# A decoder step on one core: raw weight halves loaded two weights ahead, in a ring of four

## The chip, the core and the metric

The kernel runs on one core of a Trainium2 chip. The metric is the device time of one execution in microseconds; the verdict on a change goes by the median of several. Engines are named as in the profile: PE is TensorE, DVE is VectorE, ACT is ScalarE, POOL is GpSimd, and SP is SyncE, which here issues every DMA.

## What is computed

One inference step of a decoder with two layers, for a prompt of 1024 tokens and 8 sample sequences of 4 tokens each, 1056 columns in all, with a model width of 1024. Layer 0 is a gated linear recurrence, layer 1 an attention over keys and values that three groups of heads share; each is followed by the same MLP. Everything is in float32.

```python
for layer in range(DEPTH):                      # DEPTH = 2
    if layer < N_A_LAYERS:
        h, s_fin = _hgrn2(_rmsnorm(x, a_norm[layer]), a_w_in[layer], ...)
    else:
        kv = _rmsnorm(x, kv_norm) @ w_kv        # keys, values of 3 groups
        q = _rmsnorm(x, b_norm[j]) @ b_w_q[j]   # 3 groups x 8 heads x 128
        ...
        h = o @ b_w_o[j]
    x = x + h
    x = x + jnp.square(jax.nn.relu(_rmsnorm(x, mlp_norm[layer]) @ mlp_w_up[layer])) @ mlp_w_down[layer]
```

The MLP's inner width is 4096.

## The kernel before, in words

**Weights.** A weight here is a tile of 1024 x 128 numbers, in SBUF 128 partitions x 8 x 128. `weight_order` lists all 212 of them in the order of their use. A product is made three times over (`mm3`, lines 185 to 187, and `mmx`, lines 805 to 807): each operand is split into a high part that TensorE takes as it is and a low part that holds the rest, and high x high, high x low and low x high are summed in PSUM. So each weight has to be prepared before use. `_prep` (line 125) allocates its pair `whi` and `wlo` from the pool `wp`, which has two buffers of each, loads the raw weight in two halves of 256 KB (line 146, tiles `wraw`, a ring of two), multiplies them by a norm gain for the projections of the attention (line 148, on POOL), copies each half into `whi` (line 131, on ACT) and subtracts on POOL to get `wlo` (line 132).

**When a weight is made.** `wnext` hands out the weight that is due and sees to it that this one and the next have been prepared (`wahead`). So weight i+1 is prepared when weight i begins to be used. The tracing order isn't the order on the chip: at the end a list scheduler puts every engine's instructions in an order, by priorities and by its own estimate of when operands will be there. `_prep` runs with a priority 400 instructions ahead of its place. On the chip each engine takes its queue strictly in that order and waits where an operand is late.

**The MLP.** `mlp` (line 700) goes in eight groups of 512 inner columns. For each it makes four weights `up` (`proj`, three chunks of 384, 384 and 288 columns: chunks 0, 1 and 2 below) and evacuates each chunk by a chain in `ev_up`: ReLU from PSUM on ACT (line 720), square on DVE (line 721), for some chunks differences of such results (lines 726 and 743, DVE), and the split into high and low part (line 709 on ACT, line 710 on DVE or POOL). Each group's four weights `down` come after the first `up` of the next group. For seven of the eight groups of a layer these products are made for two column chunks at a time with seven half products in place of eight (`down`, line 809), which needs sums and differences of quarters of the weight and of the hidden values. Such weights are marked `two`. Their `_prep` adds lines 152 to 165, with a priority 20 ahead: three sums on DVE (lines 159 to 161), one on POOL (line 162) into two tiles `wsum` (two buffers in all), and their split into `whix` and `wlox` (two buffers of each, in the pool `wx`), again by lines 131 and 132. Line 159 reads the second raw half.

**Inside `down`.** TensorE makes a product into the PSUM tile A, then into C and B, then comes back to A. Before it may write A again, DVE must have added A into the residual `xr` (line 819, `add(0, 0, A)`); the same holds later for the other tiles. The last group of a layer uses plain products (lines 788 to 797).

**Other users of weights.** `phase_a` (line 288) begins with the loads of the input in three chunks and prepares weights 0, 1 and 2 between them (line 293); it computes the norm, the projections and, in lanes that are stepped by `tick`, the recurrence. `phase_c` (line 860) projects keys, values and queries, attends, merges and projects back.

Of the kernel before, what the change touches and what calls it, by code (L numbers as in the profile page):

```python
# [10 lines left out]
F32 = mybir.dt.float32  # L11
# [7 lines left out]
P = 128  # L19
# [27 lines left out]
class Kern:  # L47
    def __init__(self, nc, tc, aps, ctx):
        self.nc, self.tc, self.a, self.ctx = nc, tc, aps, ctx
        self.const = ctx.enter_context(tc.tile_pool(name="const", bufs=1))  # L50
        self.rs = ctx.enter_context(tc.tile_pool(name="rs", bufs=2))
        self.op = [self.const.tile([P, KD, NT], F32R, name=n) for n in ("opH", "opL")]
        self.chunks = CHUNKS
        self.wp = ctx.enter_context(tc.tile_pool(name="wp", bufs=2))
        self.pp = ctx.enter_context(tc.tile_pool(name="pp", bufs=4, space=PSUM))
        self.pg = ctx.enter_context(tc.tile_pool(name="pg", bufs=4, space=PSUM))
        self.wx = None
        self.wt = {}
        self.wi = 0
        self.wq = self.weight_order()  # L60
        self.queue, self.lanes = deque(), []
        self.merged = 0
        self.every, self.ticks = 0, 0
        self.rawx = False
        self.fine = False
# [30 lines left out]
    def weight_order(self):  # L96
# [25 lines left out]
        mlp(1)  # L122
        return q

    def _prep(self, i):
        nc = self.nc
        src, gi, x, *two = self.wq[i]
        pool, s = (self.wx, "x") if x in (True, "p") else (self.wp, "")

        def pair(hi, lo, j, raw):  # L130
            nc.scalar.activation(hi[:, j:j + 4, :], raw, AF.Copy)  # L131
            nc.gpsimd.tensor_tensor(lo[:, j:j + 4, :], raw, hi[:, j:j + 4, :].bitcast(F32), op=ALU.subtract)  # L132

        with self.tc.high_priority(offset=400 if i > 1 else 0):
            if x == "q":

                hi, lo = (self.cp.tile([P, NP_], F32, name="q", bufs=6).bitcast(F32R).rearrange("p (k m) -> p k m", m=P)
                          for _ in range(2))
            else:
                hi = pool.tile([P, 8, P], F32R, name="whi" + s)  # L140
                lo = pool.tile([P, 8, P], F32R, name="wlo" + s)
            raws = []
            for j in (0, 4):
                raw = (self.wx if x is True and self.rawx else self.wp).tile([P, 4, P], F32, name="wraw")
                raws.append(raw)
                nc.sync.dma_start(raw, src[:, j:j + 4, :])
                if gi is not None:
                    nc.gpsimd.tensor_tensor(raw, raw, self.gains[:, gi, j:j + 4][:, :, None].to_broadcast([P, 4, P]), op=ALU.mult)  # L148
                pair(hi, lo, j, raw)
            self.wt[i] = (hi, lo)  # L150
        if two:
            with self.tc.high_priority(offset=20):

                sh = self.wx.tile([P, 8, P], F32R, name="whix")
                sl = self.wx.tile([P, 8, P], F32R, name="wlox")
                (a11, a12), (a21, a22) = ((r[:, :2], r[:, 2:]) for r in raws)
                t, u = (self.wx.tile([P, 4, P], F32, name="wsum") for _ in range(2))
                tt = nc.vector.tensor_tensor
                tt(t[:, :2], a21, a22, op=ALU.add)  # L159
                tt(t[:, 2:], t[:, :2], a11, op=ALU.subtract)  # L160
                tt(u[:, :2], a11, a21, op=ALU.subtract)
                nc.gpsimd.tensor_tensor(u[:, 2:], a12, t[:, 2:], op=ALU.subtract)  # L162
                pair(sh, sl, 0, t)
                pair(sh, sl, 4, u)
                self.wt[i] = (hi, lo), (sh, sl)
# [6 lines left out]
    def wnext(self):  # L172
        i = self.wi
        self.wi += 1
        self.wahead(i)
        self.wahead(i + 1)
        return self.wt.pop(i)


# [1290 lines left out]
```

## Time and profile before

| | us |
|---|---|
| median of 3 runs | 3045.53 |
| lowest and highest run | 3034.98, 3046.78 |
| the profiled execution | 3045.13 |
| its span, first to last instruction | 3043.4 |
| TensorE busy in the span | 2875.0 (94%) |
| VectorE, ScalarE, GpSimd busy | 1796.0, 1282.9, 1338.3 |
| mean granted TensorE clock | 0.989 of full speed |

The rows come from the profiled execution, so sums over its rows are made against its own 3045.13 us; the median lies 0.40 above. Times in timelines count from the start of the span. Busy time of an engine says how much work lies on it, and not what another engine waits for; that is read from the waits and the timelines. TensorE's matmuls overlap each other, so a matmul's row lasts longer than the distance to the next one.

### The profile page before, as it was taken

What the parts mean: (1) busy time and instruction counts of PE and PEld (TensorE: products, weight loads), DVE (VectorE), ACT (ScalarE), POOL (GpSimd) and SP (SyncE); (2) the same over time, 40 slices, a digit from 0 to 9 for tenths busy, and PEclk for the clock granted to TensorE, in tenths of its full rate; (3) what the DMA queues carried; (4) which work ended last, traced back from release to release, by engine and by line L of the source; (5) the groups of instructions that cost most, each with busy time, mean ns of one, the idle gap of its engine ahead of it and who ended that gap; (6) DMA issues with size and microseconds to landing.
All of it is one profiled execution on the core that took longest, in us unless ns stands there. A gap on an engine that the chain in (4) does not pass through costs nothing.

```text
span 3043.4 us, 47407 instructions
## 1 busy us (share of the span) xinstructions
PE 2875.0 (94%) x18144; PEld 2757.8 (91%) x18144; DVE 1796.0 (59%) x3467; ACT 1282.9 (42%) x2972; POOL 1338.3 (44%) x1149
## 2 busy tenths in 40 slices
PE   6998999889999999999899999999999999999999
PEld 5888888889999999999899889889888999999999
DVE  8777777876544455543654565665676455544442
ACT  6555656643332222332445544555544223332221
POOL 5444444453544444544463553333225445444442
PEclk9999999999999999999999999999999999999999
DMA  3100211230111111112212233332641111111112
GB/s 113 36 30 30 71 40 29 69 123 18 46 49 43 49 46 46 49 43 63 84 62 68 84 99 108 124 117 71 195 150 42 44 48 49 42 46 46 49 49 86
DMA packets 131956, 201.92 MB, mean 66 GB/s; under 512 B 26320, under 2 KB 65872, under 8 KB 129680
## 3 DMA queue, kind: packets, MB, share of 16 engines
q1 hardware_dynamic: 131728, 198.88, 20.9%
q8 instruction: 143, 2.34, 0.3%
q14 instruction: 85, 0.70, 0.1%
HBM read 164.04 MB, written 34.80 MB: 65 GB/s over the span
## 4 chain that ended last, share of the span: by engine, by line
PE 56%; DVE 10%; POOL 8%; issue 7%; DMA 5%; ACT 3%; POOLq 0%; SPq 0%; DVEq 0%; ACTq 0%
PE pj L185 10%; PE pj L186 10%; PE pj L187 10%; POOL wlo L132 4%; PE pj L805 4%; PE pj L806 4%; PE pj L807 4%; DMA wraw<-w_dn 3%; PE g L806 2%; PE g L805 2%; PE g L807 2%; POOL wlox L132 2%; PE g L1143 2%; PE g L1115 1%; PE g L1130 1%
## 5 line engine op out<-in xcount | busy, mean ns | idle before, releaser
L185 PE MATMUL pj<-opH,whi 128*128 128x352 f32 (+2 forms) x3408 | 1136.7, 334 | 9.9 <-DVE xr L211 3.5
L186 PE MATMUL pj<-opL,whi 128*128 128x352 f32 (+2 forms) x3408 | 1110.1, 326 | 5.0 <-POOL opL L233 3.2
L187 PE MATMUL pj<-opH,wlo 128*128 128x352 f32 (+2 forms) x3408 | 1107.0, 325 | 2.9 <-POOL wlo L132 2.7
L132 POOL TENSOR_TENSOR wlo<-wraw,whi 128x512 fp32r<-128x512 f32 x404 | 546.5, 1371 | 913.1 <-ACT whi L131 882.1
L185 PEld LDWEIGHTS pj<-opH,whi 128*128 128x128 f32 x3408 | 645.8, 190 | 30.6 <-issue 16.9
L186 PEld LDWEIGHTS pj<-opL,whi 128*128 128x128 f32 x3408 | 646.7, 190 | 17.9 <-POOL opL L233 6.6
L187 PEld LDWEIGHTS pj<-opH,wlo 128*128 128x128 f32 x3408 | 645.6, 189 | 6.9 <-POOL wlo L132 4.1
L131 ACT ACTIVATE whi<-wraw 128x512 fp32r<-128x512 f32 x404 | 232.6, 621 | 546.6 <-PE g L806 439.9
L721 DVE TENSOR_TENSOR tmp<-tmp 128x384 f32<-128x384 f32 (+1 forms) x192 | 169.5, 883 | 311.2 <-ACT tmp L720 311.2
L819 DVE TENSOR_TENSOR xr<-xr,pj 128x384 f32<-128x384 f32 x336 | 183.7, 553 | 138.5 <-PE pj L807 138.3
L496 POOL TENSOR_TENSOR lv<-b 128x512 f32<-128x512 f32 x112 | 125.0, 1127 | 102.7 <-PE g L593 58.4
L720 ACT ACTIVATE tmp<-pj 128x384 f32<-128x384 f32 (+1 forms) x192 | 86.9, 453 | 189.3 <-PE pj L187 188.5
L132 POOL TENSOR_TENSOR wlox<-wsum,whix 128x512 fp32r<-128x512 f32 x112 | 151.0, 1368 | 0.6 <-ACT whix L131 0.6
L162 POOL TENSOR_TENSOR wsum<-wraw,wsum 128x256 f32<-128x256 f32 x56 | 43.7, 781 | 168.0 <-DVE wsum L160 153.8
L1117 DVE CUSTOM_DVE_ANT_0 pr<-g,band,rq 128x128 f32<-128x128 f32 (+1 forms) x192 | 67.9, 405 | 79.9 <-PE g L1115 76.3
L1120 ACT ACTIVATE pr<-pr,nm 128x128 f32<-128x128 f32 (+1 forms) x192 | 84.1, 440 | 68.0 <-DVE nm L1118 67.8
L148 POOL TENSOR_TENSOR wraw<-wraw,gains 128x512 f32<-128x512 f32 x72 | 91.4, 1275 | 40.0 <-DMA wraw<-w_q 33.3
L211 DVE TENSOR_TENSOR xr<-xr,pj 128x384 f32<-128x384 f32 (+1 forms) x132 | 67.2, 516 | 69.7 <-PE pj L187 37.5
L709 ACT ACTIVATE hbH<-tmp 128x384 fp32r<-128x384 f32 x106 | 54.9, 526 | 121.2 <-DVE tmp L721 72.8
L967 POOL TENSOR_TENSOR q<-q,cos 32x512 f32<-32x512 f32 x48 | 89.8, 1877 | 30.2 <-DVE rsw L966 28.9
L159 DVE TENSOR_TENSOR wsum<-wraw 128x256 f32<-128x256 f32 x56 | 23.8, 425 | 131.5 <-DMA wraw<-w_dn 131.3
L806 PE MATMUL g<-hL,whi 128*128 128x288 f32 x336 | 100.5, 299 | 0.0
(399 smaller groups left out, 5917.8 us busy)
## 6 DMA issues: line engine op xcount, KB each, us to landing
wraw<-w_up SPq DMA_DIRECT2D x128, 256.0 KB, 2.8
wraw<-w_dn SPq DMA_DIRECT2D x128, 256.0 KB, 2.8
wraw<-w_in SPq DMA_DIRECT2D x64, 256.0 KB, 2.8
wraw<-w_q SPq DMA_DIRECT2D x48, 256.0 KB, 2.9
ub<-us SPq DMA_DIRECT2D x32, 256.0 KB, 2.2
cc<-ck SPq DMA_DIRECT2D x8, 1024.0 KB, 5.1
cc<-cv SPq DMA_DIRECT2D x8, 1024.0 KB, 5.4
wraw<-w_kv SPq DMA_DIRECT2D x24, 256.0 KB, 2.9
```

The costliest lines, as they stand in the source:

```text
L131: nc.scalar.activation(hi[:, j:j + 4, :], raw, AF.Copy)
L132: nc.gpsimd.tensor_tensor(lo[:, j:j + 4, :], raw, hi[:, j:j + 4, :].bitcast(F32), op=ALU.subtract)
L148: nc.gpsimd.tensor_tensor(raw, raw, self.gains[:, gi, j:j + 4][:, :, None].to_broadcast([P, 4, P]), op=ALU.mult)
L185: nc.tensor.matmul(ps, wh[:, kw, :], xh[:, kx, :], start=(i == 0), stop=False)
L186: nc.tensor.matmul(ps, wh[:, kw, :], xl[:, kx, :], start=False, stop=False)
L187: nc.tensor.matmul(ps, wl[:, kw, :], xh[:, kx, :], start=False, stop=(i == len(ks) - 1))
L496: nc.gpsimd.tensor_tensor(r(lv), r(b), r(b)[:, :, h - 1:h].to_broadcast([P, 256 // h, 2 * h]), op=ALU.subtract)
L721: nc.vector.tensor_tensor(r, r, r, op=ALU.mult)
L805: nc.tensor.matmul(ps, wh[:, kw, :], xh, start=start and i == 0, stop=False, skip_group_check=True)
L806: nc.tensor.matmul(ps, wh[:, kw, :], xl, start=False, stop=False, skip_group_check=True)
L807: nc.tensor.matmul(ps, wl[:, kw, :], xh, start=False, stop=stop and i == len(items) - 1, skip_group_check=True)
L819: self.nc.vector.tensor_tensor(x(i, c), x(i, c), ps, op=ALU.add)
```

## The change

The ring of raw halves has four buffers instead of two, in whichever pool it is taken from. The loading of a raw weight moves out of `_prep` into `_load`, which is called from two places: from `_prep`, where it hands out halves that were loaded before or loads them, and from `wnext`, which now loads the raw halves of weight i+2, with a priority 400 ahead, when it hands out weight i. Weights that carry a mark for another pool (the third field of their entry: `True`, `"p"` or `"q"`) are not loaded ahead. Nothing else in the preparation of a weight changes: the copies, subtractions, sums and their priorities stay where they are.

```diff
@@ -55,7 +55,7 @@
         self.wx = None
-        self.wt = {}
+        self.wt, self.raw = {}, {}
         self.wi = 0
@@ -122,6 +122,17 @@
+    def _load(self, i):
+
+        if i in self.raw:
+            return self.raw.pop(i)
+        src, _, x = self.wq[i][:3]
+        raws = []
+        for j in (0, 4):
+            raws.append((self.wx if x is True and self.rawx else self.wp).tile([P, 4, P], F32, name="wraw", bufs=4))
+            self.nc.sync.dma_start(raws[-1], src[:, j:j + 4, :])
+        return raws
+
     def _prep(self, i):
@@ -139,11 +150,8 @@
-            raws = []
-            for j in (0, 4):
-                raw = (self.wx if x is True and self.rawx else self.wp).tile([P, 4, P], F32, name="wraw")
-                raws.append(raw)
-                nc.sync.dma_start(raw, src[:, j:j + 4, :])
+            raws = self._load(i)
+            for j, raw in zip((0, 4), raws):
                 if gi is not None:
@@ -174,6 +182,10 @@
         self.wi += 1
         self.wahead(i)
         self.wahead(i + 1)
+        j = i + 2
+        if j < len(self.wq) and not self.wq[j][2]:
+            with self.tc.high_priority(offset=400):
+                self.raw[j] = self._load(j)
         return self.wt.pop(i)
```

## Rows read from the trace of the kernel before

**Rows 1.** The page, busy us, share of the span and instructions of TensorE
```profile
PE 2875.0 (94%) x18144; PEld 2757.8 (91%) x18144; DVE 1796.0 (59%) x3467; ACT 1282.9 (42%) x2972; POOL 1338.3 (44%) x1149
```

**Rows 2.** Busy time by stage: window, its length, PE, PEld, DVE, ACT, POOL, clock, DMA
```profile
0.00:100.00 100.00, 71.53 (x392) 64.59 (x393) 84.84 (x136) 60.98 (x139) 52.18 (x50) 0.95 0.31 97
...
780.00:1370.00 590.00, 570.95 (x3522) 567.00 (x3521) 297.46 (x502) 176.95 (x352) 278.19 (x237) 0.99 0.15 47
...
1450.00:2110.00 660.00, 633.73 (x4162) 584.26 (x4161) 377.53 (x861) 334.08 (x876) 295.67 (x214) 0.99 0.29 92
...
2340.00:2935.00 595.00, 577.57 (x3564) 573.93 (x3563) 301.78 (x510) 177.64 (x354) 282.34 (x239) 0.99 0.15 47
```

**Rows 3.** Waits of TensorE: us in total, times, longest us
```profile
PE pj L805 <- DVE xr L819: 36.5, 26, 1.9
...
PE pj L187 <- POOL wlo L132: 2.7, 2, 1.8
```

**Rows 4.** Timeline of TensorE, first and last `down` stalls: start, us, instruction, idle before
```profile
798.00 0.34 PE L187 MATMUL pj<-opH,wlo 128*128 128x384 f32 x1
...
804.33 0.34 PE L807 MATMUL pj<-hbH,wlox 128*128 128x384 f32 x1
806.35 0.44 PE L805 MATMUL pj<-hqH,whix 128*128 128x384 f32 x1 [1.69 <-DVE xr L819]
...
814.14 0.45 PE L805 MATMUL pj<-hqH,whix 128*128 128x384 f32 x1 [1.20 <-DVE xr L819]
...
2919.00 0.44 PE L805 MATMUL pj<-hqH,whix 128*128 128x384 f32 x1 [0.95 <-DVE xr L819]
...
2926.56 0.44 PE L805 MATMUL pj<-hqH,whix 128*128 128x384 f32 x1 [0.98 <-DVE xr L819]
```

**Rows 5.** Waits of VectorE: us in total, times, longest us
```profile
DVE wsum L159 <- DMA wraw<-w_dn: 131.3, 48, 4.2
```

**Rows 6.** Timeline of VectorE around the first two `down` of the first group
```profile
798.32 0.43 DVE L159 TENSOR_TENSOR wsum<-wraw 128x256 f32<-128x256 f32 x1 [1.78 <-DMA wraw<-w_dn]
798.66 0.55 DVE L721 TENSOR_TENSOR tmp<-tmp 128x384 f32<-128x384 f32 x1
...
801.56 1.56 DVE L721 TENSOR_TENSOR tmp<-tmp 128x384 f32<-128x384 f32 x1 [1.67 <-ACT tmp L720]
803.22 1.46 DVE L726 TENSOR_TENSOR tmp<-tmp 128x384 f32<-128x384 f32 x1
...
805.75 0.55 DVE L819 TENSOR_TENSOR xr<-xr,pj 128x384 f32<-128x384 f32 x1
...
811.69 0.43 DVE L159 TENSOR_TENSOR wsum<-wraw 128x256 f32<-128x256 f32 x1 [2.87 <-DMA wraw<-w_dn]
```

**Rows 7.** Timeline of ScalarE in the same stretch
```profile
796.46 0.47 ACT L720 ACTIVATE tmp<-pj 128x384 f32<-128x384 f32 x1
...
801.05 0.47 ACT L720 ACTIVATE tmp<-pj 128x384 f32<-128x384 f32 x1
804.72 0.52 ACT L709 ACTIVATE hpH<-tmp 128x384 fp32r<-128x384 f32 x1 [3.19 <-DVE tmp L726]
```

**Rows 8.** Timeline of GpSimd in the same stretch
```profile
801.43 2.84 POOL L132 TENSOR_TENSOR wlox<-wsum,whix 128x512 fp32r<-128x512 f32 x2
805.84 2.75 POOL L132 TENSOR_TENSOR wlo<-wraw,whi 128x512 fp32r<-128x512 f32 x2 [1.57 <-ACT whi L131]
```

**Rows 9.** Waits of the DMA queue on SyncE: us in total, times, longest us
```profile
SPq L146 <- POOL wlo L132: 1792.0, 401, 46.3
```

**Rows 10.** The page, DMA issues: count, KB each, median us from issue to landing
```profile
wraw<-w_dn SPq DMA_DIRECT2D x128, 256.0 KB, 2.8
```

**Rows 11.** Timeline of SyncE's queue at the start of the kernel
```profile
6.24 0.44 SPq L292 DMA_DIRECT2D xr<-xP  x1
11.66 0.34 SPq L146 DMA_DIRECT2D wraw<-w_in  x1
```

**Rows 12.** Waits of GpSimd: us in total, times, longest us
```profile
POOL wraw L148 <- DMA wraw<-w_q: 33.3, 28, 2.5
```

## The prediction

> **What bounds the kernel now.** I read the page's busy times first: TensorE (PE) is busy 2875.0 of 3043.4 us [rows 1], so no change to the loading of weights can win more than the 168 us in which PE stands still. The table by stage tells where these lie [rows 2]: 28.5 us at the start, 19.1 and 17.4 in the two MLP stages (780 to 1370 and 2340 to 2935), 26.3 in the stage of the projections and the attention (1450 to 2110), the rest mostly in the recurrence and at the changes of stage. Then I asked what PE waited for. One row stands out [rows 3]: line 805, the first matmul of a product in `down`, waited 26 times for the addition into xr of line 819 (VectorE, DVE), 36.5 us in all, and that is all the idle time of both MLP stages (19.1 + 17.4). On a weight itself PE waited only 2.7 us, twice, both in the first 100 us.
>
> PE's timeline shows the 26 as a pattern that repeats in each of the 14 groups of the two MLPs [rows 4]. In the first `down` of a group PE stops before its fourth product (1.69 us at 806.35; 14 times, the last 0.95, together 23.0). I call this stall A. In the second `down` it stops again (1.20 us at 814.14; 12 times, the last 0.98, together 13.4). This is stall B.
>
> Next, what held DVE, because it runs its queue in order. The list of its waits has the row: line 159, the first sum of a `two` weight, waited 48 times for the DMA of its raw half, 131.3 us [rows 5]. The timelines of DVE, ACT and POOL around the first group join this to the stalls [rows 6 to 8]. Before A, DVE has nothing to do from 796.54 to 798.32 but wait for raw halves. Behind it stands line 721 of chunk 0, whose input ACT had ready at 796.93; it runs at 798.66. So ACT's line 709 comes late, behind it ACT's two whix copies, and the ReLU of chunk 1 (line 720) starts at 801.05, although PE had finished that chunk at 798.34 (798.00 + 0.34). Lines 721 and 726 of chunk 1 now run under POOL's pair of wlox passes (801.43 to 804.27) and take 1.56 and 1.46 us, while the same line 721 takes 0.55 where POOL is idle (798.66). The add of the first product comes at 805.75 and ends 806.30. PE could have gone on at 804.67 (804.33 + 0.34). Before B it is simpler: line 159 waits 2.87 us at the head of DVE's queue, and the adds of line 819 stand behind it.
>
> **The change, part by part.**
>
> *Loads one weight earlier, ring of four.* The load of weight i+1 today waits until POOL has passed weight i's raw halves: SyncE (SP) waited 401 times for that [rows 9]. Afterwards the load of i+2 waits for the same pass of weight i, from the same call of `wnext` and with the same priority, so it stands in SP's queue where the load of i+1 stood. Nothing else on SP is moved back, and POOL issues no DMA. A raw half then lies ready for about one weight's PE time, some 10 us, where today it lands as it is wanted; a landing takes 2.8 us [rows 10]. Added instructions: none but the two of the next part.
>
> *Stall A.* Take the DMA wait away and leave the order of all queues as it is: everything from 798.32 on comes 1.78 us earlier, the add ends at 806.30 - 1.78 = 804.52, before 804.67. A is gone with 0.15 us to spare. If the sums move forward too, as their data allow, ACT takes chunk 1's ReLU at 798.4, and the ReLU's 0.47, 0.55 for each of the three DVE instructions and 0.52 for line 709 bring the chain to 801.0; then the add waits only for its product. Either way 23.0 us come back. What is late next is that add behind its own product, with more than a microsecond in hand. Bounds: 0 and 23.0; I take 23.0.
>
> *Stall B.* Without 2.87 us of waiting the adds end that much earlier, and PE has waited only 1.20 us for them. 13.4 us come back; bounds 0 and 13.4; I take 13.4.
>
> *The third weight loaded twice.* `phase_a` has prepared weights 0 to 2 before the first `wnext`, so the first call loads weight 2 again, and nobody reads it: two more DMAs of 256 KB, at 2.8 us each 5.6 us of traffic at worst in the way of the first inputs. Against that, SP today stands still from 6.68 to 11.66 before the load of weight 1, with the inputs of the last chunk behind it [rows 11]; a ring of four ends this wait of 5.0 us. The start is paced by the norm on DVE and ACT, so I take 0, with ends at -5 and +5.6.
>
> *The other stages.* In the recurrence stage nothing waits for a raw half; weights wait for their whi buffer. In the attention stage POOL's line 148 waited 33.3 us for w_q halves [rows 12]; that goes, but PE waited for no weight there, so what covers it is POOL's own slack: 0, with ends 0 and -2.7 (all that PE ever waited for wlo). The extra 4 KB of SBUF per partition issue nothing.
>
> **Sum.** The profiled execution took 3045.1 us (span 3043.4 and 1.7 around it), 0.4 below the median of the three runs. 3045.1 - 23.0 - 13.4 = 3008.7, and 0.4 for the median: **3009 us**.
>
> **Rivals.**
>
> *The wait moves along with the sums, A stays.* The order of the queues is planned on estimated times, and 48 of the 56 sums stand in DVE's queue before their data are there. With earlier loads, the sum of the weight after next could stand where the waiting sum stands now, just before line 721 of chunk 0, with POOL's passes again over chunk 1. Then only B goes: 3045.5 - 13.4 = 3032. For it: a wait of 1.8 to 4.2 us at every group's start is what the planner's estimates give today. Against it: the whix copies of that weight can't follow, since their buffer is still read by PE in the first `down`, so ACT and POOL would be free for chunk 1. A rule speaks for this rival. By the Trainium skill (SBUF — State Buffer, section Who interferes with whom), a DVE instruction with two SBUF inputs and a GpSimd instruction that reads SBUF exclude one another, and the later one waits for the whole of the earlier. By that rule POOL's unchanged passes must fall on some DVE instructions, and where these are chunk 1's again the time would be this rival's 3032 rather than 3009. The trace agrees as far as it goes: 1.56 and 1.46 us against 0.55 [rows 6, 8]. Chance 0.13.
>
> *A new wait for POOL takes its place (slower).* There are two wsum buffers for two tiles per weight, so a sum must wait until POOL has made wlox of the weight before. Were the second `down`'s successor summed so early that its line 159 stood ahead of A's add, and were POOL to take the wlo pair first and wlox after it, then: wlo would start at 805.84 less the 3.19 us that ACT idled before 804.72, so 802.65; 2.75 and 2.84 us bring POOL to 808.24, the sum and the add (0.43 + 0.55) to 809.2; PE waits 4.5 us instead of 1.69. In 14 groups 63 us, in place of 36.5: 3072. It decides only if both orders turn; today DVE never waits for POOL at these lines, all 131.3 us are DMA. Chance 0.10.
>
> *Nothing to measure.* The earlier arrival is used nowhere, because buffers of whi and wsum and not the raw halves set when a weight can be made: 3045. Against it stand 131.3 us of waits that name the DMA. Chance 0.05.
>
> **How the numbers follow.** The forecast, both stalls gone, has 0.60, with 3000 to 3018 as its own range (below it the start's 5.0, the 2.7 and the rounding; above it the start's 5.6 and a sixth of A). Half of A or of B left, 3018 to 3030, has 0.12. About 0.5% (15 us) is what a measurement of this kernel can tell from no change, so faster means below 3030.3. The first two cases are faster, 0.72, and a quarter of the first rival, where a little of A goes too, 0.03: 0.75. The rest of that rival and the third, 0.15, are within. Slower is 0.10. A range from 3000 to 3034 holds the forecast, the half cases and the first rival, 0.85 less what misses its edges.
>
> **What would show it.** Right: the row of line 159 waiting for w_dn falls from 131.3 us to a small part; line 805 waiting for line 819 falls from 36.5 to under 6; PE's busy time stays near 2875 and PE is over 99% busy in both MLP stages; 66 loads of w_in instead of 64. Wrong: A still there in each group (first rival), DVE's line 159 waiting for POOL's wlox (second), or time lost in a stage that has no stall of this kind today, the recurrence above all, because the planner set other instructions in another order.

## The result, and the profile after

The change made the kernel slower: a median of 3062.04 us (3056.77 to 3072.7, 5 runs) against 3045.53 for the kernel before, a ratio of 1.0066 with a 95% interval of 1.0038 to 1.0093. The prediction was 3009 us and a gain. The profiled execution took 3062.04 us, its span is 3060.3. Line numbers are 8 to 12 higher than before: the first sum is line 167, the sum on POOL line 170, the first matmul of a product in `down` line 817, the add into xr line 831, the square 733, the differences 738 and 755.

The page's busy times, after (those of before are [rows 1]):

```profile
PE 2881.1 (94%) x18144; PEld 2760.9 (90%) x18144; DVE 1827.5 (60%) x3467; ACT 1277.5 (42%) x2972; POOL 1338.7 (44%) x1149
```

The table by stage, after, with the columns of [rows 2]:

```profile
0.00:100.00 100.00, 74.47 (x405) 66.32 (x406) 87.00 (x139) 61.71 (x140) 51.67 (x50) 0.95 0.33 107
780.00:1370.00 590.00, 568.21 (x3508) 564.13 (x3507) 304.75 (x498) 172.19 (x351) 275.05 (x231) 0.99 0.15 46
1450.00:2110.00 660.00, 632.74 (x4148) 583.52 (x4147) 380.87 (x855) 330.81 (x864) 289.73 (x212) 0.99 0.29 92
2340.00:2935.00 595.00, 572.45 (x3534) 568.54 (x3533) 307.31 (x500) 175.16 (x355) 278.94 (x235) 0.99 0.15 46
```

The loss lies in the two MLP stages, where the gain was to come from: TensorE is busy 2.7 and 5.1 us less there than in [rows 2]. The start is better, by 2.9 us of busy time. In boundaries that both traces have: the first add of `down` starts at 804.6 instead of 805.7 (-1.1); from it to the first store of `xsp`, which follows the first MLP, 653.6 us pass instead of 647.2 (+6.4); from there to the second MLP's first add 916.9 instead of 913.9 (+3.0); from there to the end 685.2 instead of 676.6 (+8.6). The sum is the 16.9 us by which the span grew.

TensorE's waits, after (us in total, times, longest; [rows 3] before):

```profile
PE pj L817 <- DVE xr L831: 48.9, 26, 2.3
```

VectorE's waits, after ([rows 5] before):

```profile
DVE wsum L167 <- DMA wraw<-w_dn: 123.8, 42, 4.1
...
DVE wsum L167 <- POOL wlox L143: 39.7, 14, 2.8
```

Three things are to be seen. TensorE's wait for the adds grew from 36.5 to 48.9 us, the +12.4 that make up most of the loss. VectorE's wait for the raw halves, 131.3 us before, is almost as long as it was. And there is a row that was not there: the first sum waits 14 times, once in each group, for POOL's `wlox`.

The order in which VectorE's queue has the sums S0 to S3 of a group's four `down` weights, and the adds A0, A1 of line 831 (819) of its first two `down`, tells why. It is fixed when the program is built:

```
before   S0 S1 | A0 x4  S2  A0 x3 | A1 x3  S3  A1 x4
after    S0 S1 S2 | A0 x7 | S3  A1 x7
```

With the loads one weight earlier, the scheduler set the sums a weight earlier as well: S2 ahead of the whole first `down`, S3 ahead of the first add of the second. Timelines of the third group after show what each costs. VectorE, at the first `down` (start, us, instruction, idle before):

```profile
972.40 0.43 DVE L167 TENSOR_TENSOR wsum<-wraw 128x256 f32<-128x256 f32 x1 [4.01 <-DMA wraw<-w_dn]
...
986.40 0.42 DVE L167 TENSOR_TENSOR wsum<-wraw 128x256 f32<-128x256 f32 x1 [2.24 <-DMA wraw<-w_dn]
...
988.27 0.71 DVE L733 TENSOR_TENSOR tmp<-tmp 128x384 f32<-128x384 f32 x1 [0.30 <-ACT tmp L732]
989.88 0.56 DVE L738 TENSOR_TENSOR tmp<-tmp 128x384 f32<-128x384 f32 x1 [0.91 <-POOL hpL L722]
991.03 0.56 DVE L722 TENSOR_TENSOR hpL<-tmp,hpH 128x384 fp32r<-128x384 f32 x1 [0.59 <-ACT hpH L721]
991.50 0.55 DVE L831 TENSOR_TENSOR xr<-xr,pj 128x384 f32<-128x384 f32 x1
```

S1 (972.40) and S2 (986.40) still wait for their DMA, 4.01 and 2.24 us, since they too stand about one weight earlier. S2 now has the place that S1 had before, ahead of the evacuation of chunk 0, and its fourth sum on POOL stands ahead of POOL's split of chunk 0. The difference of line 738 overwrites what that split reads, so it waits 0.91 us more, and the first add is late again. GpSimd, timeline of the same stretch:

```profile
987.76 0.80 POOL L170 TENSOR_TENSOR wsum<-wraw,wsum 128x256 f32<-128x256 f32 x1 [2.72 <-DVE wsum L168]
988.52 1.33 POOL L722 TENSOR_TENSOR hpL<-tmp,hpH 128x384 fp32r<-128x384 f32 x1
```

Then the second `down` of that group. GpSimd, timeline:

```profile
994.31 0.81 POOL L722 TENSOR_TENSOR h0L<-tmp,h0H 128x288 fp32r<-128x288 f32 x1
999.37 2.54 POOL L143 TENSOR_TENSOR wlo<-wraw,whi 128x512 fp32r<-128x512 f32 x2 [4.25 <-ACT whi L142]
1001.88 2.49 POOL L143 TENSOR_TENSOR wlox<-wsum,whix 128x512 fp32r<-128x512 f32 x2
```

ScalarE, timeline of the same stretch:

```profile
998.66 1.15 ACT L142 ACTIVATE whi<-wraw 128x512 fp32r<-128x512 f32 x2 [4.99 <-PE g L818]
999.72 1.14 ACT L142 ACTIVATE whix<-wsum 128x512 fp32r<-128x512 f32 x2
```

VectorE, timeline of the same stretch:

```profile
1003.18 1.47 DVE L167 TENSOR_TENSOR wsum<-wraw 128x256 f32<-128x256 f32 x1 [2.85 <-POOL wlox L143]
1004.58 0.54 DVE L831 TENSOR_TENSOR xr<-xr,pj 128x384 f32<-128x384 f32 x1
```

TensorE, timeline of both `down`:

```profile
992.11 0.44 PE L817 MATMUL pj<-hqH,whix 128*128 128x384 f32 x1 [1.32 <-DVE xr L831]
...
1005.17 0.44 PE L817 MATMUL pj<-hqH,whix 128*128 128x384 f32 x1 [2.30 <-DVE xr L831]
```

S3 needs a `wsum` buffer, and there are two for two tiles per weight; it must wait until POOL has read S2's. POOL makes that `wlox` only at 1001.88, because ScalarE's copies for the third weight wait until TensorE has finished the weight whose buffers they take (4.99 us before 998.66). S3 stands ahead of the second `down`'s first add, so TensorE stops for 2.30 us. In the trace the first `down` stops 12 times, before its fourth product, for 1.04 to 2.08 us (16.9 in all), and the second 14 times, before its fourth product too, for 2.27 to 2.30 (32.0).

Before, both stalls lay in the first `down`: 23.0 us before its fourth product and 13.4 before its seventh, the last. The timeline of TensorE before shows where the first two `down` of the first group begin, each with its first matmul on `hpH` and `whi`:

```profile
801.38 0.33 PE L805 MATMUL pj<-hpH,whi 128*128 128x384 f32 x1
...
815.29 0.33 PE L805 MATMUL pj<-hpH,whi 128*128 128x384 f32 x1
```

The stall at 814.14 in [rows 4] lies ahead of the second one. So those 13.4 us are gone, and the 32.0 us in the second `down` are new.

### The profile page after: what moved, and what is told of

The parts are those of the page before. It is cut to its first block, busy times and chain, and to the rows that moved or that the text cites. A ratio compares the mean times of both kernels' runs of the same rounds, so it can differ in the third digit from the quotient of the medians.

```text
span 3060.3 us, 47423 instructions
## 1 busy us (share of the span) xinstructions
PE 2881.1 (94%) x18144; PEld 2760.9 (90%) x18144; DVE 1827.5 (60%) x3467; ACT 1277.5 (42%) x2972; POOL 1338.7 (44%) x1149
## 5 line engine op out<-in xcount | busy, mean ns | idle before, releaser
L167 DVE TENSOR_TENSOR wsum<-wraw 128x256 f32<-128x256 f32 x56 | 38.4, 686 | 163.5 <-DMA wraw<-w_dn 123.8
L223 DVE TENSOR_TENSOR xr<-xr,g 128x288 f32<-128x288 f32 x112 | 50.9, 455 | 109.9 <-PE g L819 109.9
L817 PE MATMUL pj<-hqH,whix 128*128 128x384 f32 x184 | 65.0, 353 | 48.9 <-DVE xr L831 48.9
```

The costliest lines, as they stand in the source:

```text
L223: self.nc.vector.tensor_tensor(x, x, ps, op=ALU.add)
L817: nc.tensor.matmul(ps, wh[:, kw, :], xh, start=start and i == 0, stop=False, skip_group_check=True)
```

## The experiments

The theory at this point (theory 1): what decides is where the sums stand in the queues; the four buffers move them, and each of two sums makes a stall of its own. The main rival (theory 2): the loads ahead themselves disturb something.

**The two parts apart.** The ring of four alone, in the kernel before:

```diff
-                raw = (self.wx if x is True and self.rawx else self.wp).tile([P, 4, P], F32, name="wraw")
+                raw = (self.wx if x is True and self.rawx else self.wp).tile([P, 4, P], F32, name="wraw", bufs=4)
```

> The kernel before with the ring of raw halves at four and no load moved (weights are still loaded by _prep, when the weight before them begins to be used). Theory 1, the order: what cost the time is the planned order of DVE's queue, and the ring alone brings it about, since a load with priority 400 starts whenever a buffer is free. Then this kernel is as slow as the changed one: 3062 us within 6, with 14 waits of the sum's first line for wlox (about 40 us) and about 49 us of waits of the products' first line for the adds into xr. Theory 2, the loads: the early loading itself costs (loads two weights ahead hold SP's queue and the DMA engines). Then this kernel is like the one before: 3045 within 6, and 36 us of such waits.

Measured 3063.79 us (3060.77 to 3069.58), ratio 1.0061 (1.0048 to 1.0074). The load two weights ahead alone, in the kernel after:

```diff
-            raws.append((self.wx if x is True and self.rawx else self.wp).tile([P, 4, P], F32, name="wraw", bufs=4))
+            raws.append((self.wx if x is True and self.rawx else self.wp).tile([P, 4, P], F32, name="wraw"))
```

> The changed kernel with the ring of raw halves left at two: the load of weight i+2 is still issued by wnext, and waits for the half of weight i+1. Theory 1, the order: like the kernel before, 3045 us within 6, about 36 us of waits of the products for the adds, no wait of a sum for wlox. Theory 2, the loads: like the changed kernel, 3062 within 6.

Measured 3042.28 us (3037.15 to 3047.51), ratio 0.9991 (0.9983 to 1.0). TensorE's wait for the adds with the ring alone:

```profile
PE pj L805 <- DVE xr L819: 50.6, 27, 2.9
```

VectorE's new wait with the ring alone:

```profile
DVE wsum L159 <- POOL wlox L132: 39.7, 14, 2.8
```

TensorE's wait for the adds with the early load alone:

```profile
PE pj L817 <- DVE xr L831: 34.6, 23, 1.9
```

The ring alone is as slow as the whole change and has its new wait to the tenth of a microsecond; in the MLPs VectorE's queue has the order of the kernel after. The early load alone, with two halves, leaves the order of before there, and the time too. So the ring is the part that does it.

This doesn't yet decide between the theories, because the loads follow the ring and not the line that asks for them. SyncE's timelines show when the two halves of S2 are loaded in the third group: before, after, with the ring alone, with the early load alone.

```profile
992.99 1.80 SPq L146 DMA_DIRECT2D wraw<-w_dn  x2
...
981.84 1.89 SPq L133 DMA_DIRECT2D wraw<-w_dn  x2
...
985.93 1.91 SPq L146 DMA_DIRECT2D wraw<-w_dn  x2
...
993.70 1.79 SPq L133 DMA_DIRECT2D wraw<-w_dn  x2
```

The first add of that group starts at 991.59, 991.50, 995.58 and 992.31. So the halves are loaded 1.4 us behind the add before and with the early load alone, and 9.7 us ahead of it in the other two: the ring alone loads as early as the whole change. What early loads cost is told by the held kernels below, which have the same order with early and with late loads.

**The new wait taken away.** Four buffers for `wsum` in the kernel after:

```diff
-  t, u = (self.wx.tile([P, 4, P], F32, name="wsum") for _ in range(2))
+  t, u = (self.wx.tile([P, 4, P], F32, name="wsum", bufs=4) for _ in range(2))
```

> The changed kernel with four wsum buffers instead of two, so that the sum of a weight need not wait until POOL has made wlox of the weight before. Theory 1: the 14 waits for wlox (39.7 us) go, and with them the stalls of 2.3 us in the second down (32 us). The sum of the fourth weight then stands in the first down, where its raw half lands late, and a DMA wait takes the place: a stall of about 1.2 us per group comes back, so 3062 - 32 + 17 = 3047, and 3030 if it does not. Theory 2: 3062 within 6.

Measured 3030.69 us (3023.48 to 3039.84), ratio 0.9952 (0.9936 to 0.9969): 31 us below the kernel after. The profiled execution was the slowest of the six, 3039.84 us. TensorE's wait for the adds:

```profile
PE pj L817 <- DVE xr L831: 29.7, 25, 2.4
```

VectorE's waits at the first sum, all of them:

```profile
DVE wsum L167 <- DMA wraw<-w_dn: 160.9, 56, 4.1
```

The row of `wlox` is gone. All 56 first sums now wait for their DMA instead: the scheduler took this freedom too and set S3 into the first `down`, ahead of its fifth add. The stall that the expectation feared there did come, 13 times before the seventh product (13.4 us); the other 12 lie before the fourth (16.3 us). That the time is nevertheless the 3030 us of the other branch is luck. The expectation left out the half-clock stretches of TensorE, which the last section prices and of which this trace has 2 instead of 6; they are part of the difference, and the rest stays open.

**The order taken from the scheduler.** The sums of the second, third and fourth weight are queued behind the first add of the `down` in which they are asked for, with an ordering edge on that add. The sums move from `_prep` into a method of their own, unchanged; the core of it:

```diff
+    def sums(self, ins=None):
...
+        with (self.tc.issue_after(ins.ins) if ins is not None else nullcontext()), self.tc.high_priority(offset=20):
...
+                    self.hold = True
                     for p in range(4):
                         self.down(2 * p, self.wnext(), hs, hb)
+                    self.hold = False
...
-        add(0, 0, A)
+        self.sums(add(0, 0, A))
```

The queue is then S0 | A0, S1, A0 x6 | A1, S2, A1 x6 | and so on. First in the kernel after:

> The changed kernel with the three DVE sums of the second, third and fourth down weight of a group queued behind the add of the first product of the down before (an issue order on DVE alone, no wait). Theory 1: no sum stands ahead of an add for which PE waits, no sum waits for the DMA or for wlox inside a down, so both stalls go: the products' wait for the adds falls from 48.9 us to under 8, and the time to about 3062 - 45 = 3017, between 3008 and 3025. Theory 2: the time stays at 3062 within 10, since the loads are the same.

Measured 2996.97 us (2994.42 to 2999.99), ratio 0.9842 (0.9829 to 0.9855). Its two MLP stages in the table by stage:

```profile
780.00:1370.00 590.00, 590.00 (x3675) 588.94 (x3675) 306.65 (x524) 184.65 (x360) 289.24 (x243) 1.00 0.16 49
...
2340.00:2935.00 595.00, 595.00 (x3706) 593.96 (x3706) 303.00 (x519) 182.26 (x354) 290.01 (x243) 1.00 0.16 49
```

TensorE never stops there. The expectation had the sign, but its 3017 us was 20 too high and the time lies below its range; the last section says where part of the rest came from. Then the same edges in the kernel before, with its two halves and no early load, and in the kernel before with four halves:

> The kernel before (ring of two halves, loads one weight ahead), with the sums of the second, third and fourth weight of each group of four put into the queues behind the first add of the down before. Theory 1 (where the sums stand decides, not when the halves land): the 36.5 us of waits of the products for the adds go, with some 7 us of half-clock stretches that lie in those stages, so 3045 - 44 = 3001 (2994 to 3010), as with four halves. Theory 2 (the ring and the early load are needed once the order is right): with two halves the load of the third weight starts only when POOL has passed the second, so the sum waits for the DMA in the middle of a down, the adds behind it come late again, 1.2 us or more in each of 42 places: 3020 to 3050.

Measured 2999.3 us (2998.14 to 3000.07), ratio 0.9852 (0.9837 to 0.9867).

> The kernel before with a ring of four halves, no load two weights ahead, and the sums held as in the run before. Theory 1: as the held kernel with both parts of the change, 2997 (2992 to 3004), the early load being worth nothing in the MLP stages. Theory 2: the early load is needed: 3010 or more.

Measured 2997.24 us (2990.05 to 2998.79), ratio 0.9841 (0.9823 to 0.9859). The three held kernels can't be told apart: their intervals overlap. SyncE's load of S2's halves in the third group, in the held kernel after and in the held kernel before:

```profile
970.25 1.79 SPq L134 DMA_DIRECT2D wraw<-w_dn  x2
...
986.71 1.51 SPq L147 DMA_DIRECT2D wraw<-w_dn  x2
```

The group's first add starts at 980.86 and 984.11, so the loads are 10.6 us early in the one and 2.6 us late in the other. The time is the same either way, and the loss is gone although the loads are early: theory 2 falls here. VectorE's wait at the first sum is that of S0 alone, 14 times. With two halves:

```profile
DVE wsum L174 <- DMA wraw<-w_dn: 58.3, 14, 4.2
```

With four halves and the early load:

```profile
DVE wsum L182 <- DMA wraw<-w_dn: 36.9, 14, 3.4
```

More buffers and earlier loads do shorten that wait, by 21 us, and this is worth nothing, because TensorE has work while it lasts. With the order put right the change is not needed at all.

**One sum at a time.** In the held version of the kernel after, the mark is set for one weight only.

```diff
-                    self.hold = True
                     for p in range(4):
+                        self.hold = p == 2
```

> The kernel after, only the fourth weight's sum held, behind the first add of the third down. Theory 1 (two separate stalls, each made by the one sum that stands ahead of its add): the 2.3 us stall of the second down goes in all 14 groups (32 us), the 1.0 to 2.1 us stall of the first down stays (17 us): 3062 - 32 = 3030 (3022 to 3038), DVE no longer waits for wlox at the first sum. Rival (the wait only moves to the third down): 3055 or more, with stalls of 2 us there.

Measured 3016.38 us (3013.65 to 3019.24), ratio 0.9908 (0.9893 to 0.9923). With `p == 1` in its place, the third weight's sum:

> The kernel after, only the third weight's sum held, behind the first add of the second down; the fourth weight's sum then stands three instructions behind it, ahead of three adds. Theory 1: the stall of the first down goes (17 us), but wlox of the third weight is now made later, the fourth's sum waits for it longer, and the stall of the second down grows from 2.3 to between 2.3 and 5 us in each of 14 groups: 3045 to 3085, say 3060; DVE's wait for wlox grows from 39.7 us. Rival (the wait for wlox costs little, the DMA waits ahead of chunk 1 make the loss): 3035 or less.

Measured 3004.89 us (3000.28 to 3007.66), ratio 0.9874 (0.9856 to 0.9891). TensorE's wait for the adds with S3 alone held:

```profile
PE pj L834 <- DVE xr L848: 17.7, 13, 2.5
```

With S2 alone held:

```profile
PE pj L834 <- DVE xr L848: 6.6, 15, 0.5
```

With S3 held the 32 us of the second `down` are gone and 17.7 remain, about the 16.9 of the first: the stalls are two, as theory 1 says, and the time fell further than the 32 us, to below the expected range. With S2 held the expectation failed, by 40 us at least: the stall of the second `down` did not grow, it all but vanished. The time is that of the rival, by which the wait for `wlox` costs little. VectorE's timeline there, in the third group:

```profile
991.15 0.55 DVE L848 TENSOR_TENSOR xr<-xr,pj 128x384 f32<-128x384 f32 x1 [0.49 <-PE pj L836]
991.62 0.90 DVE L182 TENSOR_TENSOR wsum<-wraw 128x256 f32<-128x256 f32 x1
...
995.32 1.50 DVE L182 TENSOR_TENSOR wsum<-wraw 128x256 f32<-128x256 f32 x1 [1.20 <-POOL wlox L174]
```

The wait for `wlox` is still there, 1.20 us, but S3 now stands behind the third add of the second `down` instead of ahead of its first. The expectation priced how late `wlox` is made and not which add stands behind the wait. The rival is right for this place only: ahead of the first add the wait for `wlox` cost the 32.0 us that went with S3 held. Of two waits of one length the one ahead of the first add costs more: 2.85 us there cost 2.30 us of TensorE (1003.18 and 1005.17 after), 2.87 us ahead of the fifth add 1.20 (811.69 and 814.14 before, [rows 4, 6]). Here, ahead of the fourth, 1.20 us of waiting and 1.50 of sum cost at most 0.5.

## Why the prediction was wrong

**The loads.** That the load of weight i+2 would take the place of that of i+1 was right, and so were the 66 loads of w_in. The step that failed is the next one, "a raw half then lies ready for about one weight's PE time, some 10 us": it took the sums to stay where they were. They moved by the same weight, and the wait for the halves went from 131.3 only to 123.8 us.

**Stall A.** "Take the DMA wait away and leave the order of all queues as it is" is the failed step: neither held. The second branch, "if the sums move forward too", named the move and still got 23.0 us back; it left out the wait for the DMA that S2 brings with it to that place, and that line 726's difference (738 after) overwrites in place what POOL's split reads (0.91 us in the row at 989.88). Of 23.0 us 6.1 came back.

**Stall B.** The prediction read it as a stall of the second `down`; it lay before the last product of the first, behind S2's wait for its DMA ahead of the fifth add. There the 13.4 us did come back, but not because the wait ended: S2 left that place and took a wait of 2.24 us along (986.40). What failed is that the step took the 2.87 us out with nothing in their stead. S3's wait of 2.85 us for `wlox` came, ahead of the first add of the second `down`, and its stalls of 32.0 us stand in the sum as nothing. The stalls then add up: 36.5 - 6.1 - 13.4 + 32.0 = 49.0, against 48.9 in the row.

**The rivals.** The slower one was the right mechanism, the two `wsum` buffers and a sum ahead of an add, with 0.10. Its place was wrong (the first `down`, with S2; it was the second, with S3), and its price was 4.5 us per group instead of 2.3. What the prediction held against the first rival, that the `whix` copies can't follow early since TensorE still reads their buffer, was true, and is just why `wlox` came late: the argument against one rival was the mechanism of the other, and the two were never put together. The first rival happened as well: S2 moved to just before chunk 0's square, most of A stayed, and B went. As to the rule it cited, from the Trainium skill (SBUF — State Buffer, section Who interferes with whom): the sum that begins at 1003.18 under POOL's `wlox` takes 1.47 us against 0.42 at 986.40, which agrees with it. By these two rows the slower sum would be 1.05 of the 2.30 us, an estimate; no run here separates this from the rest of the stall.

**The small terms.** The weight that is loaded twice and the start: -1.1 us to the first add, taken as 0, inside its ends of -5 and +5.6. The other stages: +3.0 us, taken as 0, outside its ends of 0 and -2.7. The held kernel after, with loads as early, takes 912.9 us there, 1.0 less than the kernel before, so where the 3.0 us come from stays open. The chances were wrong in the same way as the sum: 0.72 rested on two stalls going together, and both hung on the one assumption that earlier data leave the plan alone.

## What to carry to other kernels

Where a scheduler plans the queues on estimated landings, a buffer more can be a change of order first: here it moved instructions ahead to where the plan believed their data, and the engine then waited there with everything behind it. So ask of a wait not only what ends it but what is queued behind it, and try an ordering edge behind the critical instruction before more buffers; here it gave 1.5% with the old ring, and the new ring added nothing. A wait is priced by the instruction right behind it: 2.85 us ahead of a first add cost 2.30 us of TensorE, 2.87 us ahead of a fifth one 1.20.

## What the runs showed of the hardware

A short stop of TensorE can cost more than its length. After the stall that ends at 818.28 in the kernel after, the granted clock falls to half, the level of 1.2 GHz, and comes back within 6 us. Windows of 2 us there, columns as in [rows 2]:

```profile
818.00:820.00 2.00, 1.72 (x10) 1.72 (x11) 2.00 (x5) 0.00 (x0) 0.74 (x1) 0.91 0.00 0
820.00:822.00 2.00, 2.00 (x10) 2.00 (x10) 0.65 (x2) 0.00 (x0) 0.00 (x0) 0.50 0.00 0
822.00:824.00 2.00, 2.00 (x11) 2.00 (x11) 0.65 (x2) 0.00 (x0) 0.00 (x0) 0.74 0.00 0
824.00:826.00 2.00, 2.00 (x16) 2.00 (x15) 0.92 (x2) 0.00 (x0) 0.00 (x0) 1.00 0.00 0
```

Matmuls of 288 columns start 0.24 us apart there and 0.13 apart at full clock:

```profile
821.19 0.44 PE L819 MATMUL g<-hH,wlo 128*128 128x288 f32 x1
821.43 0.44 PE L817 MATMUL g<-hH,whi 128*128 128x288 f32 x1
...
825.31 0.30 PE L819 MATMUL g<-hH,wlo 128*128 128x288 f32 x1
825.44 0.30 PE L817 MATMUL g<-hH,whi 128*128 128x288 f32 x1
```

In the MLP stages such a stretch follows 4 of the 26 stalls of the kernel before and 6 of the 26 after, each time within 3 us of the stall's end; in the held kernel above, which has no stall there, the clock shows 1.00 in both stages. The counts are of one profiled execution of each kernel. By the clock column 0.09, 0.50 and 0.26 of 2 us each are lost in the one above, 1.7 us; at that price they cost 6.8 us before and 10.2 after. Stalls and stretches together account for the MLP stages: +12.4 + 3.4 = 15.8 us against the 15.0 lost by the change, and 36.5 + 6.8 = 43.3 against the 42.0 that the held kernel gains on the kernel before (from the first add to the `xsp` store 624.9 us instead of 647.2, and from the second MLP's first add to the end 656.9 instead of 676.6). Its expectation, and that with S3 held alone, came out too high in part because the stalls were counted there without these stretches; with S3 held one of the 6 is left. Why one stall has a stretch behind it and the next of the same length has none, no run here tells.
